# One layer of a hybrid decoder trunk: ones' products among the first products, recurrent outputs by tokens, and a last operand made between products

## The chip, the cores and the metric

The kernel runs on one core of a Trainium2 chip. Times are microseconds (us) on the device, from launch to end; the time of a kernel is the median of its runs. The engines are TensorE (PE; PEld is its loading of weights), VectorE (DVE), ScalarE (ACT), GpSimd (POOL) and SyncE (SP), which issues most transfers.

## The reference

Input x has 1024 tokens of 1024 channels, float32; there is one layer. In short:

```
u    = rms_norm(x)
proj = u @ w_in                          # q, k, v: 8 heads of 64; hq, hf, hi, hg: 4 heads of 128
attn = rms_norm(three dilated windows of causal attention, merged by their sums)
# recurrence, per head, in chunks: forget = lb + (1-lb)*sigmoid(hf); key = 1-forget; b = cumsum(log forget)
A       = causal(q*exp(b) @ (key*exp(-b)).T)
o       = A @ hi + (q*exp(b)) @ state;   state = exp(b_end)*state + (key*exp(b_end-b)).T @ hi
rec  = rms_norm(o, over the 128 channels of a head) * silu(hg)
h    = x + concat(attn, rec) @ w_out
g, v = rms_norm(h) @ w_up                # 2 x 2816 columns
h    = h + (gelu(causal conv of width 3 over g) * v) @ w_down
out  = rms_norm(h)
```

## The kernel before, in words

**Layout.** Most tensors lie with channels on the 128 partitions and tokens along the row: 8 channel blocks of 1024 tokens, worked in two halves of 512 tokens. To hold float32 accuracy each operand of a large product is split into an upper part in a shortened format and the lower rest, so that one product becomes three: upper by upper, upper by lower, lower by upper.

**Weights.** `Ring` (L48) brings weights in pieces of 128x512 in the order of a plan: a transfer by SP into one of five raw buffers, the upper part by ACT (L86), the lower part by POOL or, for keys listed in `ring.on_vector`, by DVE (both L88). Five split pieces live at a time; `done` frees one and starts the next.

**Order.** PE's instructions run in the order in which the program writes them. The other engines' queues are ordered by a planner that uses the written order and its own costs, except where an instruction is pinned (`keep_in_program_order`, `pin`). Work is woven by hand: generators yield a product's price in us, and `Fill.run(us)` plays as many products as the credit pays for.

**Stages.**
- *Start.* Eight ones' products (L378), then the queries and keys of heads 0 and 1, `dense` (L445 to L458), channel block by channel block as x arrives and is split by `scale_x` (ACT L390, DVE L391). `rms1` (L404) sums the squares by a ones' product (L406, and L409 by columns); its result R1 scales what comes out of PSUM. For half 1 it is called after the first three value products (`tok`, L460 to L473), and the half-1 copies of queries and keys of heads 0 and 1 (`evac` in `qk_half`, L530 to L546) come at once after it.
- *Attention.* For each head and each pair of 128-token blocks j, `score_steps` makes scores (L575, L576), DVE masks them and finds the maximum (L578), ACT exponentiates (L583), POOL divides (L587); `value_steps` turns them by PE (L602 to L609), splits them (ACT L613, DVE L614) and multiplies by the values (L621 to L625). Beside each head run weight products from `beside`; the loop's `cost[h]` says how many us of them a head gets.
- *Recurrence.* `recur` (L838 to L914) is one turn for one head and one half: five steps, eight turns, played between the products of hf, hq and hg at places given by `steps` in units of 5.2 us. Step 1 makes the cumulative sums and exponentials; step 2 turns B (psK, L865) and makes psA (L870 into the lower 64 rows, L873 into the upper); step 3 makes psU (L882) and the states; step 4 makes the outputs psO (L901, L903), channels by tokens, and their squares; step 5 sums the squares over the channels by a ones' product (L908), takes the root (`rstd_part`, L325 to L332, on 128x512) and multiplies by the gate (L910 on DVE, L912 on POOL).
- *Output product.* `out_pair` (L990 to L1026): two of eight output blocks at a time, PSUM banks of the tag mm, two in number; DVE adds x (L1014). The second norm (`norm2`, L1038) runs between.
- *Up.* Column blocks 0 and 1 are plain. From block 2 on, `up` (L1220) makes a block by seven products instead of eight (a Strassen-Winograd form): the activations' operands b11, b21, b22 and T1 to T4 are made once, the weights' s1 to s4 per block on DVE by `Mix`. T4, the operand that meets a22, is made by `sum_4` (L1176) and `split` (L1158) before block 2.
- *Down.* The same form over ten pairs of blocks, then the final norm.

PSUM has eight banks: the tags mm, s, o and t with two each until the up stage.

Of the kernel before, what the change touches and what calls it, by code (L numbers as in the profile page):

```python
# [22 lines left out]
NH = 8  # L23
# [179 lines left out]
def hybrid_kernel(ctx: ExitStack, tc: tile.TileContext, xT, w_qk, w_tok, w_hg, w_out, w_up,  # L203
# [173 lines left out]
    for _ in range(8):  # L377
        PE.matmul(warm[:, :P], ones, ones, start=True, stop=True)  # L378
# [66 lines left out]
    def dense(key, hf, evac, last, tag="mm"):  # L445
# [3 lines left out]
        for c in range(NCT):  # L449
            hi, lo = ring.get((key, c // 4))  # L450
            s = slice((c % 4) * P, (c % 4 + 1) * P)
            PE.matmul(ps, hi[:, s], uhi[:, c, t], start=(c == 0), stop=False)
# [66 lines left out]
    if True:  # L519
# [181 lines left out]
        cost = {h: 4.8 * (4 if h in (5, 6) else 3) for h in range(NH)}  # L701
        for h in range(NH):
            fill.add(*beside[h])
            for j in range(4):
# [7 lines left out]
                k = 0  # L712
                while True:
# [5 lines left out]
                    if not got or k % 2:  # L719
                        more = next(va, 0)  # L720
# [23 lines left out]
    with pool("hg", "right") as hg:  # L744
# [93 lines left out]
        def recur(h, hf):  # L838
# [29 lines left out]
            for c in range(4):  # L868
                s, s1 = slice(c * P, (c + 1) * P), slice(c * P, c * P + 64)
                PE.matmul(psA[0:64, s], B[:, s1], E[:, s], start=True, stop=True)  # L870
            for c in range(4):
                s, s2 = slice(c * P, (c + 1) * P), slice(c * P + 64, (c + 1) * P)
# [7 lines left out]
            for c in range(4):  # L880
# [3 lines left out]
            DVE.tensor_mul(U, psU.rearrange("p (c v) -> p c v", c=4), ex[:, 8:12].unsqueeze(2).to_broadcast([P, 4, P]))  # L884
# [5 lines left out]
            for c in range(1, 4):  # L890
                DVE.scalar_tensor_tensor(U[:, c], U[:, c - 1], ex[:, 4 + c : 5 + c], U[:, c], op0=ALU.mult, op1=ALU.add)
# [4 lines left out]
            yield  # L896
            psO = bank("o", f"psO{nm}")
            for c in range(4):
                s = slice(c * P, (c + 1) * P)
                no_state = hf == 0 and c == 0  # L900
                PE.matmul(psO[:, s], iv[:, 4 * hf + c, h * P : (h + 1) * P], AT[:, c], start=True, stop=no_state)  # L901
# [3 lines left out]
            ACT.activation(sq, psO, AF.Square)  # L905
            yield
            ss = bank("t", f"hss{nm}")
            PE.matmul(ss, ones, sq, start=True, stop=True)  # L908
            R = rstd_part(ht("rs_y", f"rhy{nm}"), ht("rs_m", f"rht{nm}"), ss, 1.0 / P)
            DVE.scalar_tensor_tensor(R, psO, col(V_HG + h), R, op0=ALU.mult, op1=ALU.mult)  # L910
            g_ = G[h, hf]
            POOL.tensor_mul(g_, R, g_)  # L912
# [38 lines left out]
        for n, (h, hf) in enumerate(((0, 0), (0, 1), (1, 0), (1, 1), (2, 0), (3, 0), (2, 1), (3, 1))):  # L951
# [3 lines left out]
            steps += zip((start, at, at + 1, at + 2.2, at + 3.1), rec_steps(h, hf))  # L955
# [34 lines left out]
        def out_pair(hf, d0):  # L990
# [217 lines left out]
    for c in range(KS):  # L1208
        sum_4(c)
    T[4] = operand(1, KS, "b12")  # L1210
    for c in range(KS):
        split(T[4][c], uf1[c])
    ps1_cm.__exit__(None, None, None)

    with pool("ps2", "left", space=PSUM) as ps2:
# [4 lines left out]
        def up(f, sums):  # L1220
# [6 lines left out]
            for i in (1, 2, 5, 6, 7, 4, 3) if f == 2 else (1, 5, 6, 7, 2, 3, 4):  # L1227
# [31 lines left out]
        sums = iter(())  # L1259
# [234 lines left out]
```

## Time and profile before

| what | value |
|---|---|
| median of 3 runs | 1224.47 us (1224.36 to 1224.59) |
| the profiled execution's own time | 1229.3 us |
| its span, first to last instruction | 1227.1 us |
| PE busy | 1205.3 us, 98% of the span |
| DVE busy | 964.7 us, 79% |
| ACT busy | 633.2 us, 52% |
| POOL busy | 309.1 us, 25% |
| mean granted clock of TensorE | 0.993 |

In a row of the waits stand who waited, for whom, the total, the count and the longest. In a row of the windows stand the stretch, its length, then for each engine asked for the busy time with the instructions in brackets, the granted clock, the transfers' share and GB/s. In a row of the timeline stand the start, the duration, the engine and line, what is written from what, sizes, the count, and in brackets the idle time before it with what ended it. In the chain of waits stand the start, the part on the chain and the instruction. The profiler models the ends of products: a 128x512 product is shown with 0.39 us while the next starts after 0.23.

### The profile page before, as it was taken

How to read it: one execution, taken by the hardware profiler on the slowest of the kernel's cores; microseconds unless marked ns; L12 is line 12 of the kernel's file. 1: busy time of each engine (PE TensorE's matmuls, PEld its weight loads, DVE VectorE, ACT ScalarE, POOL GpSimd, SP SyncE). 2: the span in 40 equal slices, each digit the busy share in tenths (PEclk: the TensorE clock that was granted, in tenths of full speed). 3: DMA queues.
4: the chain of work that ended last, by engine and by line, in shares of the span. 5: the costliest groups of instructions: out<-in, count | busy, mean ns of one | idle time of the engine just before them, and what ended most of it. 6: DMA issues, size and time to landing. Idle time of an engine off the chain costs nothing.

```text
span 1227.1 us, 17373 instructions
## 1 busy us (share of the span) xinstructions
PE 1205.3 (98%) x5992; PEld 1012.3 (82%) x5992; DVE 964.7 (79%) x1788; ACT 633.2 (52%) x1149; POOL 309.1 (25%) x286
## 2 busy tenths in 40 slices
PE   8999999999999999999999999999999999999996
PEld 7898888888888888878878888888888888888886
DVE  7867776666778877474988988988988879957996
ACT  7466667667656656454633334334434354444553
POOL 1154446555011024513212223122222210000000
PEclk9999999999999999999999999999999999999998
DMA  6121112123111112343012233332233257434522
GB/s 235 42 70 53 52 53 78 60 65 111 52 35 48 57 60 96 120 137 112 26 61 88 93 109 117 118 111 80 102 112 120 104 173 264 155 104 154 172 96 94
DMA packets 71816, 122.38 MB, mean 100 GB/s; under 512 B 7344, under 2 KB 17840, under 8 KB 71728
## 3 DMA queue, kind: packets, MB, share of 16 engines
q1 hardware_dynamic: 60928, 101.80, 25.8%
q10 hardware_dynamic: 10800, 19.47, 4.1%
q8 instruction: 47, 0.77, 0.3%
q14 instruction: 41, 0.34, 0.1%
HBM read 97.65 MB, written 23.59 MB: 99 GB/s over the span
## 4 chain that ended last, share of the span: by engine, by line
PE 90%; DVE 4%; issue 2%; ACT 2%; DMA 0%; POOL 0%; SPq 0%; DVEq 0%; ACTq 0%; POOLq 0%
PE p L1105 10%; PE p L1104 10%; PE p L1103 10%; PE ds L1394 3%; PE ds L1392 3%; PE ds L1393 3%; PE da L1394 2%; PE da L1392 2%; PE da L1393 2%; PE po L1007 2%; PE po L1009 2%; PE po L1008 2%; PE piv L504 1%; PE S L575 1%; PE piv L506 1%
## 5 line engine op out<-in xcount | busy, mean ns | idle before, releaser
L88 POOL TENSOR_TENSOR wlo<-raww,whi 128x512 fp32r<-128x512 f32 x141 | 206.7, 1477 | 388.7 <-ACT whi L86 259.5
L86 ACT CAST whi<-raww 128x512 fp32r<-128x512 f32 x276 | 167.8, 617 | 188.1 <-DVE raww L120 61.5
L88 DVE TENSOR_TENSOR wlo<-raww,whi 128x512 fp32r<-128x512 f32 x136 | 100.1, 736 | 18.2 <-ACT whi L86 18.0
L86 ACT CAST whi<-r 128x512 fp32r<-128x512 f32 x70 | 43.6, 623 | 83.0 <-PE ds L1393 49.7
L587 POOL TENSOR_SCALAR P<-P,st 128x512 f32<-128x512 f32 (+2 forms) x96 | 55.7, 591 | 112.8 <-DVE st L584 65.7
L578 DVE CUSTOM_DVE_ANT_0 P<-S,mask 128x512 f32<-128x512 f32 (+2 forms) x96 | 52.0, 553 | 28.0 <-PE S L576 27.2
L583 ACT ACTIVATE P<-P,st 128x128 f32<-128x128 f32 (+3 forms) x64 | 49.7, 776 | 33.8 <-DVE st L582 17.0
L614 DVE TENSOR_TENSOR tl<-T,th 128x512 fp32r<-128x512 f32 (+1 forms) x80 | 50.8, 635 | 18.2 <-ACT th L613 17.0
L88 DVE TENSOR_TENSOR wlo<-r,whi 128x512 fp32r<-128x512 f32 x70 | 47.9, 685 | 18.7 <-ACT whi L86 18.5
L1394 PE MATMUL ds<-fhi,wlo 128*128 128x512 f32 x160 | 62.3, 389 | 0.0
L1393 PE MATMUL ds<-flo,whi 128*128 128x512 f32 x160 | 62.3, 389 | 0.0
L1392 PE MATMUL ds<-fhi,whi 128*128 128x512 f32 x160 | 62.2, 389 | 0.0
L1103 PE MATMUL p<-b1h,whi 128*128 128x512 f32 x160 | 62.2, 389 | 0.0
L1104 PE MATMUL p<-b1l,whi 128*128 128x512 f32 x160 | 62.2, 389 | 0.0
L1105 PE MATMUL p<-b1h,wlo 128*128 128x512 f32 x160 | 62.2, 389 | 0.0
L1132 ACT ACTIVATE cv<-cv 128x512 f32<-128x512 f32 x44 | 27.8, 633 | 61.6 <-DVE cv L1125 61.4
L1366 POOL TENSOR_TENSOR facc<-facc,sqf 128x256 f32<-128x256 f32 x4 | 2.9, 737 | 222.8 <-ACT sqf L1365 222.8
L1125 DVE SCALAR_TENSOR_TENSOR cv<-g,vec,cv 128x511 f32<-128x511 f32 (+2 forms) x92 | 55.0, 603 | 4.7 <-ACT cv L1122 3.7
L613 ACT CAST th<-T 128x512 fp32r<-128x512 f32 (+1 forms) x80 | 43.0, 537 | 22.3 <-PE T L606 17.9
L88 DVE TENSOR_TENSOR flo<-rawf,fhi 128x512 fp32r<-128x512 f32 x70 | 47.9, 684 | 3.7 <-ACT fhi L86 3.7
L86 ACT CAST fhi<-rawf 128x512 fp32r<-128x512 f32 x70 | 43.2, 617 | 14.6 <-DMA rawf<-spT 5.6
L1392 PE MATMUL da<-fhi,whi 128*128 128x512 f32 x120 | 46.7, 389 | 0.0
(669 smaller groups left out, 3864.2 us busy)
## 6 DMA issues: line engine op xcount, KB each, us to landing
raww<-in_w_up_dram SPq DMA_DIRECT2D x88, 256.0 KB, 3.1
raww<-in_w_tok_dram SPq DMA_DIRECT2D x52, 256.0 KB, 2.6
rawf<-spT SPq DMA_DIRECT2D x40, 256.0 KB, 2.7
r<-in_w_down_dram SPq DMA_DIRECT2D x40, 256.0 KB, 3.2
raww<-in_w_hg_dram SPq DMA_DIRECT2D x32, 256.0 KB, 2.6
raww<-in_w_out_dram SPq DMA_DIRECT2D x32, 256.0 KB, 2.6
spB<-a ACTq DMA_DIRECT2D x30, 256.0 KB, 2.3
spT<-t ACTq DMA_DIRECT2D x30, 256.0 KB, 2.0
```

The costliest lines, as they stand in the source:

```text
L86: self.pin(self.high(hi[:, :w], raw))
L88: self.pin(low.tensor_sub(lo[:, :w], raw, f32(hi[:, :w])))
L578: DVE.tensor_tensor_reduce(Pt[:, k0 : k0 + w], S[:, :w], mask[:, m : m + w], -1.0, BIG * 3, op0=ALU.add, op1=ALU.min, accum_out=st[:, k0 / ...
L587: POOL.tensor_scalar(e, e, st[:, 3:4], 1.0, op0=ALU.mult, op1=ALU.mult)
L614: DVE.tensor_sub(tl[:, :n], T[:, :n], f32(th[:, :n]))
L1103: PE.matmul(ps, hi[:, s], bhi, start=(start and n == 0), stop=False)
L1104: PE.matmul(ps, hi[:, s], blo, start=False, stop=False)
L1105: PE.matmul(ps, lo[:, s], bhi, start=False, stop=(stop and n == len(rhs) - 1))
L1125: DVE.scalar_tensor_tensor(dst, x, col(V_CW + j * NFF + f), dst, op0=ALU.mult, op1=ALU.add)
L1392: PE.matmul(ps[d], hi[:, s], ahi, start=(k == 0), stop=False)
L1393: PE.matmul(ps[d], hi[:, s], alo, start=False, stop=False)
L1394: PE.matmul(ps[d], lo[:, s], ahi, start=False, stop=(k == NPAIR - 1))
```

## The change

- *Start.* Ones' products are put among the first products of queries and keys: four after the first product of channel block 0 of head 0, one after its third, two after the first of channel block 1.
- *Half 1's sum.* The scores of head 0, block pair 0, and the fourth value product come ahead of `rms1(1)`. The copies of the half-1 queries and keys of heads 0 and 1 move into the loop of head 0, at block pairs 0 and 1.
- *Last head.* Its share of weight products is 12.8 us instead of 14.4, and 1.6 us are played ahead of its last block pair.
- *Recurrence.* In psA the products into lower and upper rows alternate chunk by chunk. In half 1 the fourth chunk of psU, which nothing reads, is left out. The outputs come with tokens on the partitions (operands swapped); ACT sums the squares along the row, four instructions of 128 columns with a sum each; the root is taken on 128x4; DVE multiplies; at step 5 four transposes turn the result, and DVE multiplies by weight and gate. Step 5 moves from 3.1 to 3.7 units.
- *Banks.* In half 1 the output blocks 0 and 1 use the tag s, 2 and 3 the tag o, 6 and 7 the tag s.
- *Block 2.* T4 is made one channel block after each of the first four products. The product with a22 comes last and the one with s4 sixth, in the ring's plan as well.

```diff
-            xs = ("a11", "a12", "s1", "s2", "s3", "a22", "s4") if f == 2 else ("a11", "s1", "s2", "s3", "a12", "s4", "a22")
+            xs = ("a11", "a12", "s1", "s2", "s3", "s4", "a22") if f == 2 else ("a11", "s1", "s2", "s3", "a12", "s4", "a22")
...
+    def busy(n):
+        for _ in range(n):
+            PE.matmul(warm[:, :P], ones, ones, start=True, stop=True)
+
+    busy(8)
+
+    between = {(("qk", 0), 0, 0): (4, 1), (("qk", 0), 0, 1): (2, 0)}
...
+            b = between.get((key, hf, c), (0, 0))
             PE.matmul(ps, hi[:, s], uhi[:, c, t], start=(c == 0), stop=False)
+            busy(b[0])
             PE.matmul(ps, hi[:, s], ulo[:, c, t], start=False, stop=False)
             PE.matmul(ps, lo[:, s], uhi[:, c, t], start=False, stop=(c == NCT - 1))
+            busy(b[1])
...
-        rms1(1)
-        for g in pairs[1]:
-            next(g, None)
...
+        for Ps in score_steps(0, 0):
+            pass
+        fill.add(v0[3])
+        fill.run()
+        rms1(1)
...
-        fill.add(v0[3])
-        fill.run()
-        for Ps in score_steps(0, 0):
-            pass
         fill.add(v0[4])
...
         cost = {h: 4.8 * (4 if h in (5, 6) else 3) for h in range(NH)}
+        cost[NH - 1] = 12.8
...
+                if (h, j) == (NH - 1, 3):
+                    fill.run(1.6)
...
+                        if h == 0 and k == 1 and j < 2:
+                            next(pairs[1][j], None)
                         more = next(va, 0)
...
                 PE.matmul(psA[0:64, s], B[:, s1], E[:, s], start=True, stop=True)
-            for c in range(4):
-                s, s2 = slice(c * P, (c + 1) * P), slice(c * P + 64, (c + 1) * P)
                 PE.matmul(psA[64:128, s], B[:, s2], E[:, s2].unsqueeze(1).to_broadcast([P, 2, 64]), start=True, stop=True)
...
-            for c in range(4):
+            n = 3 if hf else 4
+            for c in range(n):
                 s = slice(c * P, (c + 1) * P)
                 PE.matmul(psU[:, s], kT[:, s], iv[:, 4 * hf + c, h * P : (h + 1) * P], start=True, stop=True)
...
-                PE.matmul(psO[:, s], iv[:, 4 * hf + c, h * P : (h + 1) * P], AT[:, c], start=True, stop=no_state)
+                PE.matmul(psO[:, s], AT[:, c], iv[:, 4 * hf + c, h * P : (h + 1) * P], start=True, stop=no_state)
                 if not no_state:
-                    PE.matmul(psO[:, s], st[:, c], E[:, s], start=False, stop=True)
-            sq = ht("rs_m", f"hsq{nm}")
-            ACT.activation(sq, psO, AF.Square)
+                    PE.matmul(psO[:, s], E[:, s], st[:, c], start=False, stop=True)
+            sq, ss = ht("rs_m", f"hsq{nm}"), hg.tile([P, 12], F32, tag="sm", name=f"hss{nm}", bufs=2)
+            for c in range(4):
+                s = slice(c * P, (c + 1) * P)
+                ACT.activation(sq[:, s], psO[:, s], AF.Square, accum_out=ss[:, c : c + 1])
+            R = rstd_part(ss[:, 4:8], ss[:, 8:12], ss[:, 0:4], 1.0 / P)
+            on = ht("rs_y", f"on{nm}")
+            DVE.tensor_mul(on.rearrange("p (c v) -> p c v", c=4), psO.rearrange("p (c v) -> p c v", c=4),
+                           R.unsqueeze(2).to_broadcast([P, 4, P]))
             yield
-            ss = bank("t", f"hss{nm}")
-            PE.matmul(ss, ones, sq, start=True, stop=True)
-            R = rstd_part(ht("rs_y", f"rhy{nm}"), ht("rs_m", f"rht{nm}"), ss, 1.0 / P)
-            DVE.scalar_tensor_tensor(R, psO, col(V_HG + h), R, op0=ALU.mult, op1=ALU.mult)
+            psT = bank("t", f"psT{nm}")
+            for c in range(4):
+                s = slice(c * P, (c + 1) * P)
+                PE.transpose(psT[:, s], on[:, s], ident)
             g_ = G[h, hf]
-            POOL.tensor_mul(g_, R, g_)
+            DVE.scalar_tensor_tensor(g_, psT, col(V_HG + h), g_, op0=ALU.mult, op1=ALU.mult)
...
-            steps += zip((start, at, at + 1, at + 2.2, at + 3.1), rec_steps(h, hf))
+            steps += zip((start, at, at + 1, at + 2.2, at + 3.7), rec_steps(h, hf))
...
-                    ps[d] = bank("mm", f"po{hf}_{d}")
+                    ps[d] = bank({(1, 0): "s", (1, 2): "o", (1, 6): "s"}.get((hf, d0), "mm"), f"po{hf}_{d}")
...
-    for c in range(KS):
-        sum_4(c)
     T[4] = operand(1, KS, "b12")
-    for c in range(KS):
-        split(T[4][c], uf1[c])
+
+    def last_sums():
+        for c in range(KS):
+            sum_4(c)
+            split(T[4][c], uf1[c])
+            yield
...
-            for i in (1, 2, 5, 6, 7, 4, 3) if f == 2 else (1, 5, 6, 7, 2, 3, 4):
+            for i in (1, 2, 5, 6, 7, 3, 4) if f == 2 else (1, 5, 6, 7, 2, 3, 4):
...
-        sums = iter(())
+        sums = last_sums()
```

More of the change, by code (lines that the diff above doesn't have):

```diff
@@ L376, in hybrid_kernel @@
     warm = bank("mm", "warm")
-    for _ in range(8):
-        PE.matmul(warm[:, :P], ones, ones, start=True, stop=True)
+    def busy(n):
[3 more added lines that the diff above has]
+    between = {(("qk", 0), 0, 0): (4, 1), (("qk", 0), 0, 1): (2, 0)}
     pin = tc.keep_in_program_order
@@ L868, in recur @@
             for c in range(4):
-                s, s1 = slice(c * P, (c + 1) * P), slice(c * P, c * P + 64)
+                s, s1, s2 = slice(c * P, (c + 1) * P), slice(c * P, c * P + 64), slice(c * P + 64, (c + 1) * P)
                 PE.matmul(psA[0:64, s], B[:, s1], E[:, s], start=True, stop=True)
-            for c in range(4):
-                s, s2 = slice(c * P, (c + 1) * P), slice(c * P + 64, (c + 1) * P)
                 PE.matmul(psA[64:128, s], B[:, s2], E[:, s2].unsqueeze(1).to_broadcast([P, 2, 64]), start=True, stop=True)
@@ L883, in recur @@
             U = ht("rs_m", f"U{nm}").rearrange("p (c t) -> p c t", c=4)
-            DVE.tensor_mul(U, psU.rearrange("p (c v) -> p c v", c=4), ex[:, 8:12].unsqueeze(2).to_broadcast([P, 4, P]))
+            DVE.tensor_mul(U[:, :n], psU[:, : n * P].rearrange("p (c v) -> p c v", c=n),
+                           ex[:, 8 : 8 + n].unsqueeze(2).to_broadcast([P, n, P]))
             st = ht("rs_y", f"st{nm}").rearrange("p (c t) -> p c t", c=4)
@@ L890, in recur @@
             for c in range(1, 4):
-                DVE.scalar_tensor_tensor(U[:, c], U[:, c - 1], ex[:, 4 + c : 5 + c], U[:, c], op0=ALU.mult, op1=ALU.add)
+                if c < n:
+                    DVE.scalar_tensor_tensor(U[:, c], U[:, c - 1], ex[:, 4 + c : 5 + c], U[:, c], op0=ALU.mult, op1=ALU.add)
                 DVE.tensor_scalar_mul(st[:, c], U[:, c - 1], ex[:, c : c + 1])
```

## The prediction

> **What bounds the kernel now.** I read the page's head and its chain of work first, then what TensorE waits for, then short windows around those waits, then the recurrence's instructions one by one.
>
> ```profile
> span 1227.1 us, 17373 instructions
> PE 1205.3 (98%) x5992; PEld 1012.3 (82%) x5992; DVE 964.7 (79%) x1788; ACT 633.2 (52%) x1149; POOL 309.1 (25%) x286
> ...
> PE 90%; DVE 4%; issue 2%; ACT 2%; DMA 0%; POOL 0%; SPq 0%; DVEq 0%; ACTq 0%; POOLq 0%
> ```
>
> TensorE (PE) is busy for 98% of the span and makes 90% of the chain that ends last. So a microsecond taken out of PE's own queue is a microsecond off the time, as long as its operands come in time; work taken from another engine is worth nothing by itself. The second view lists what PE waits for (total us, times, longest).
>
> ```profile
> PE p L1105 <- POOL wlo L88: 2.4, 2, 2.2
> PE p__qk___0_0_211 L452 <- ACT uhi L390: 1.4, 1, 1.4
> PE ss L406 <- DVE sq L402: 1.4, 1, 1.4
> PE po L1007 <- DVE h L1014: 1.3, 1, 1.3
> PE T L602 <- DVE tl L614: 1.1, 1, 1.1
> PE T L603 <- POOL P L587: 0.9, 1, 0.9
> ```
>
> These six waits, 8.5 us, are each touched by an edit. Windows (length, PE busy, granted clock) show what else they cost:
>
> ```profile
> 5.30:8.70 3.40, 1.39 (x4) 1.00 0.98 338
> 8.70:12.20 3.50, 3.21 (x9) 0.51 1.04 393
> 42.90:46.30 3.40, 2.38 (x15) 1.00 0.04 7
> 46.30:49.70 3.40, 3.40 (x18) 0.50 0.00 0
> 551.40:554.90 3.50, 2.18 (x11) 1.00 0.33 107
> 630.00:633.40 3.40, 1.16 (x5) 1.00 0.00 0
> 633.40:636.80 3.40, 3.40 (x9) 0.50 0.49 155
> ```
>
> Three of the waits are each followed by 3.4 us at half clock. Half of 3.4 us is lost: 1.7 us a spell. The fourth wait, 1.3 us at 551, fell in a window with 2.18 us of work and was not punished. In the window from 42.9 the 2.38 us include eight one-column products (0.95 us); without them 1.43 us remain. So on this trace the clock fell after windows with 1.2 to 1.4 us of full products and held after one with 2.2.
>
> The Trainium skill (TensorE: Matmul & The Clock Gate, "What's actually happening") ties the cold state to at least one idle window of about 3.4 us. Here it came after waits of 1.4 to 2.4 us, so the trace disagrees; if idle windows alone decided, these spells would not hang on the waits, and would stay (a rival below).
>
> **The change part by part.**
>
> *Ones' products at the start.*
>
> ```profile
> 1.05 3.78 PE L378 MATMUL warm<-ones 128*128 128x128 f32 x16 [1.05 <-DVE ones L229]
> 12.41 0.39 PE L452 MATMUL p__qk___0_0_211<-uhi,whi 128*128 128x512 f32 x1
> ```
> ```profile
> 9.52 1.45 DVE L391 SCALAR_TENSOR_TENSOR ulo<-xt,vec,uhi 128x512 fp32r<-128x512 f32 x2
> ```
>
> The eight products that are there take 3.78 us as 16 instructions, 0.24 each. Seven more are 14 instructions, 1.5 us at full clock and 3.3 at half. They stand where PE waits for the first pieces of x, in a window that has 2.0 us free (3.40 - 1.39), so I cost them at nothing; the loss end is 3.3 - 2.0 = 1.3 us, all of them at half clock. They lift the window's 1.39 us of work to about 2.4 us (0.9 + 0.2 of ones after the first channel block, part of 0.4 after the second). That is above the 2.18 that kept the clock: the spell goes. PE's first product after the wait is at 9.0, so the spell costs (12.2 - 9.0)/2, about 1.5 us. The operands can follow: the lower part of channel block 2 is done by 11.0, where its product starts at 12.4 today. Gain **1.5** (-1.3 to 1.5).
>
> *Sums of squares later.* The ones' product that waits for DVE's sums (1.4 us) is moved behind block (0,0)'s scores and the fourth value product, 24 products of 256 columns, 0.12 each (half of a full one's 0.23, in the recurrence's chain below), so 2.9 us of PE work that cover the 1.4; the spell from 46.3 goes with it. Behind it come R1, the second half's queries and keys of head 0 and 1, moved into the loop of head 0, and the value copies, all on DVE and ACT, no transfers. Gain 1.4 + 1.7 = **3.1** (0 to 3.1). Head 0's first transposes wait 0.9 us for POOL; they start on earlier scores, but the moved copies now stand between, so I take half, **0.5** (-1 to 0.9).
>
> *Value products of the last head.* With a share of 12.8 instead of 14.4, 1.6 us of weight products are left for the place of the wait at 295. I take the wait's **1.1** (0 to 1.1).
>
> *Recurrence, eight turns.* Its chain:
>
> ```profile
> 357.25 0.86 PE hss L908 x2
> ...
> 375.50 0.44 PE psK L865 x4
> 375.94 0.69 PE psA L870 x5
> 376.96 0.49 PE psA L873 x5
> 377.45 1.06 PE hss L908 x2
> 378.51 0.23 PE p__hg___1_0_4384 L452
> ...
> 383.97 0.89 PE psU L882 x8
> ```
> ```profile
> 375.87 0.76 PE L870 MATMUL psA<-E,B 128*64 128x128 f32 x5
> 376.37 0.32 PE L873 MATMUL psA<-E,B 128*64 128x128 f32 x1
> ...
> 376.74 0.71 PE L873 MATMUL psA<-E,B 128*64 128x128 f32 x5
> ```
>
> The sum of squares over a head's channels by a ones' product costs 0.86 us of PE; four transposes of the same size as psK's cost 0.44. 8 x 0.42 = **3.4** saved. psU loses one of four chunks in half 1: 2 of 8 instructions of 0.89 us, 0.22, in four turns: **0.9**. The outputs by tokens swap the operands of products whose sizes stay (128x128), so they cost the same. In psA the products into the upper 64 rows already run beside those into the lower 64: the first L873 starts at 376.37, before L870 is through, but 0.50 us after L870's first, for it stands behind eight of them. In alternate order it stands behind two. Five of L870 start within 0.76 - 0.27 = 0.49 us, 0.12 a step, so behind two is 0.12 to 0.25; I take 0.16. That is 0.34 saved a turn, 8 x 0.34 = **2.7**. The loss end is no overlap: 16 x 0.11 (psK's) = 1.76 us against today's 1.42 (from 375.87 to the last start, 377.18, and 0.11), so +0.34 a turn.
>
> What can eat this is a new wait: the transposes need the normalised outputs, which go through ACT and DVE.
>
> ```profile
> 348.70 0.44 PE psO L901 x4
> ```
> ```profile
> 353.21 0.58 ACT L905 ACTIVATE hsq<-psO 128x512 f32<-128x512 f32 x1
> ...
> 359.58 0.68 ACT L327 ACTIVATE rht<-hss,eps 128x512 f32<-128x512 f32 x1
> ```
> ```profile
> 365.42 0.75 DVE L910 SCALAR_TENSOR_TENSOR rhy<-psO,vec,rhy 128x512 f32<-128x512 f32 x1
> ```
>
> Today the squares start about 3.0 us after psO's 14 products end at 350.2, and from the logarithm to the product's end are 6.6 us, queueing included. Four squares with sums I put at 1.6 us (0.4 each, an estimate from the 0.58 of the wide one), and five operations on 4 columns instead of 512 save some 0.4 each, 2.0: 3.0 + 1.6 + 4.6 = 9.2 us. The time there is: 1.5 steps of 5.2 us = 7.8, and the next turn's psK and psA between, 1.6: 9.4. That is a tie, so I take off 0.25 us a turn, **-2.0** (0 to -20.8: 3.0 + 2.4 + 6.6 = 12.0 without any saving, 2.6 us late). A late transpose holds up everything on PE behind it, the gate products above all. ACT gets no more work (0.58 + 3 x 0.68 = 2.6 before; 1.6 + 3 x 0.28 = 2.4 after), and the gate's product leaves POOL, with its 1.4 us, for DVE:
>
> ```profile
> L912 POOL TENSOR_TENSOR G<-rhy,G 128x512 f32<-128x512 f32 x7 | 10.0, 1435 | 81.5 <-DVE rhy L910 81.5
> ```
>
> DVE does two wide operations a turn after it (the normalising one, and the gate's) where it had three, so it is not the loser.
>
> *Banks.* The output products of half 1 get banks of their own for d 0 to 3, so the product at 553 no longer waits for DVE's addition in the middle of norm 2: **1.3** (0 to 1.3; the next use of an old bank is two pairs, 22 us, later).
>
> *Block 2's last operand.*
>
> ```profile
> 628.60 2.49 DVE L1160 TENSOR_TENSOR b12l<-uf,b12h 128x512 fp32r<-128x512 f32 x4
> ...
> 637.09 0.69 DVE L115 TENSOR_TENSOR raww<-raww,raww 128x512 f32<-128x512 f32 x1 [3.72 <-DMA raww<-in_w_up_dram]
> ```
> ```profile
> 629.24 0.62 ACT L86 CAST whi<-raww 128x512 fp32r<-128x512 f32 x1
> ```
> ```profile
> 629.93 2.89 POOL L88 TENSOR_TENSOR wlo<-raww,whi 128x512 fp32r<-128x512 f32 x1 [22.76 <-DVE b12l L1160]
> ```
> ```profile
> 600.00:616.00 16.00, 16.00 (x72) 13.26 (x71) 16.00 (x25) 7.50 (x13) 5.60 (x2) 1.00 0.14 50
> 616.00:640.00 24.00, 21.76 (x88) 17.28 (x87) 19.49 (x34) 8.55 (x15) 4.39 (x2) 0.93 0.20 67
> ```
>
> The sixth product's weights a22 are late: their upper part stands in ACT's queue behind the four pieces of T4, and POOL's lower part comes at 632.8. After the change a22 comes seventh, and T4's pieces stand between products of 2.7 us (12 x 0.23). DVE is full before it (16.00 of 16.00) and T4's last piece ends at 628.60 + 2.49 = 631.1. With s4's two operations (the sum and the lower part, 1.4 us) now ahead of it, that becomes 632.5. The sixth product could start at 629.9, when a22's upper part was there, so the seventh starts at 629.9 + 2.7 = 632.6. It just fits, piece by piece. What is late next is block 3's first mixed weights (the DVE row at 637.09, behind a transfer whose buffer a22 frees; a22 is split earlier now). Gain 2.4 + 1.7 = **4.1** (0 to 4.1).
>
> Sum: 1.5 + 3.1 + 0.5 + 1.1 + 3.4 + 0.9 + 2.7 - 2.0 + 1.3 + 4.1 = **16.6 us**. The profiled execution took 1229.3 us (span 1227.1 and 2.2 around it), so it would be 1212.7; the median of the runs is 4.8 lower, 1224.5, and the same difference gives **1207.9 us**.
>
> **Rivals.**
> *The wait moves to T4 (chance 0.12).* DVE is full there; if its queue puts T4 behind the additions of products 5 and 6 (three more, 1.8 us) and the seventh product waits 2 us, the clock falls again: the 4.1 are lost, 1212.0. For it: 16.00 of 16.00. Against: DVE sat idle 3.72 us at 637.
> *The clock is not held (0.12).* The ones do not count as enough work, or idle windows alone decide: one to three spells stay, 1.5 to 4.9 us, 1209.4 to 1212.8. Against: windows of 1.4 and 2.2 us of work fell on different sides.
> *psA's halves do not overlap when alternated (0.08).* 2 x 2.7 = 5.4: 1213.3. Against: the two rows that interleave at 376.4 to 376.7.
> *The transposes wait (slower, 0.05).* At recurrence step +3.7 PE stands for 2.6 us in each of eight turns: 18.6 gained elsewhere, 20.8 lost, 1226.7. It decides from 2.3 us a turn. For it: the 3.0 us before the squares and the 6.6 after the logarithm. Against: wide operations become narrow, and one ones' product leaves the chain.
> *Nothing happens (0.03).* Other engines' queues fall into another order and give all back: 1224.
>
> **How the numbers follow.** The forecast has 0.55 (1202.5 to 1211), two rivals at once 0.05 (to 1217). All terms at their good ends give 1203.5 (0.4 more at head 0, 2.0 at the transposes). The range 1202.5 to 1216 holds forecast and the single rivals, 0.87. A change under 0.2% (2.4 us) cannot be told from none here; faster by more 0.92, same 0.03, slower 0.05.
>
> **What would show it.** Right: clock 1.00 in the windows 8.7 to 12.2, 46.3 to 49.7 and after block 2; no PE wait on sq, on h or on wlo; L873 starting within 0.2 us of L870; no row of psT waiting for `on` above 0.3 us. Wrong: such a row with over 2 us a turn, a wait on b12 in block 2, or a half-clock window where none was.

## The result, and the profile after

The changed kernel takes **1211.64 us** (median of 4 runs, 1210.85 to 1212.4) against 1224.53 us (1224.36 to 1226.41, 4 runs) for the kernel before: ratio 0.9891, interval 0.9874 to 0.9908. The forecast was 1207.9 us with a range of 1202.5 to 1216. So the sign was right and the time lies in the range, 3.7 us above the forecast. The profiled execution of the changed kernel took 1211.85 us, near its median; the first profiled one of the kernel before took 1229.3, 4.8 above its own.

Line numbers from here on are those of the changed kernel: L380 is the ones' product (L378 before), L459, L461 and L462 the large products (L452 to L454), L584 and L587 scores and mask (L575, L578), L591 the negated maximum, L592 and L596 exponential and division (L583, L587), L611 to L615 the transposes of attention, L882 and L883 psA (L870, L873), L930 the new transposes psT.

The page of the changed kernel, its head and the head of its chain of work:

```profile
span 1209.9 us, 17468 instructions
PE 1193.9 (99%) x6014; PEld 1006.8 (83%) x6014; DVE 951.6 (79%) x1792; ACT 627.2 (52%) x1205; POOL 299.2 (25%) x278
...
PE 93%; issue 2%; DVE 2%; ACT 1%; POOL 0%; DMA 0%; SPq 0%; DVEq 0%; ACTq 0%; POOLq 0%
```

TensorE (PE) lost 11.4 us of busy time with 22 instructions more, and 5.8 us of not being busy. What it still waits for (total us, times, longest):

```profile
PE T L612 <- POOL P L596: 2.6, 1, 2.6
...
PE p L1125 <- POOL wlo L88: 0.5, 1, 0.5
```

The waits on sq and on h are gone, that on wlo in block 2 shrank from 2.4 to 0.5, and no row names psT, the tile of the new transposes. The first row is new: head 0's transposes wait 2.6 us for POOL, where it was 0.9. Windows of the changed kernel (length, PE busy, granted clock, transfers):

```profile
5.30:8.70 3.40, 3.04 (x20) 1.00 0.96 319
8.70:12.20 3.50, 3.50 (x17) 1.00 1.05 401
...
46.30:49.70 3.40, 3.40 (x28) 1.00 0.00 0
...
60.00:63.40 3.40, 0.77 (x7) 1.00 0.22 77
63.40:66.80 3.40, 3.40 (x15) 0.50 0.22 77
```

The half-clock spells at 8.7, 46.3 and after block 2 are gone, and there is one where there was none: at 63.4, behind the new wait. The prediction had named that as a sign of being wrong.

Where the time went, by the start of one marked product per stage in the timelines. "Before again" is a second profiled execution of the kernel before (1224.99 us, the first experiment below). The forecast's terms are those of the prediction, put to these stages.

| stage, from one marked product to the next | before | before again | after | after minus before / before again | forecast |
|---|---|---|---|---|---|
| start to the first sum of squares | 24.68 | 24.56 | 22.55 | -2.1 / -2.0 | -1.5 |
| to head 2's queries and keys (sum of squares, head 0) | 57.63 | 56.11 | 56.63 | -1.0 / +0.5 | -3.6 |
| to the first product of hf (last head) | 222.70 | 222.62 | 221.75 | -0.9 / -0.9 | -1.1 |
| to the first up product (recurrence, banks) | 267.07 | 267.18 | 257.77 | -9.3 / -9.4 | -6.3 |
| to the first down product (block 2) | 429.73 | 427.37 | 425.84 | -3.9 / -1.5 | -4.1 |
| to the end of the span | 225.33 | 225.33 | 225.34 | 0.0 / 0.0 | 0 |
| span | 1227.14 | 1223.17 | 1209.88 | -17.3 / -13.3 | -16.6 |

Against the execution on which the sum was made, the sum was right within 0.7 us, with two large errors of opposite sign in it. Against the second execution of the kernel before, 3.4 us of it were not there to be had.

### The profile page after: what moved, and what is told of

The parts are those of the page before. It is cut to its first block, busy times and chain, and to the rows that moved or that the text cites. A ratio compares the mean times of both kernels' runs of the same rounds, so it can differ in the third digit from the quotient of the medians.

```text
span 1209.9 us, 17468 instructions
## 1 busy us (share of the span) xinstructions
PE 1193.9 (99%) x6014; PEld 1006.8 (83%) x6014; DVE 951.6 (79%) x1792; ACT 627.2 (52%) x1205; POOL 299.2 (25%) x278
## 4 chain that ended last, share of the span: by engine, by line
PE 93%; issue 2%; DVE 2%; ACT 1%; POOL 0%; DMA 0%; SPq 0%; DVEq 0%; ACTq 0%; POOLq 0%
PE p L1125 10%; PE p L1123 10%; PE p L1124 10%; PE ds L1418 3%; PE ds L1417 3%; PE ds L1416 3%; PE po L1027 2%; PE po L1029 2%; PE po L1028 2%; PE da L1418 2%; PE da L1417 2%; PE da L1416 2%; PE S L584 1%; PE piv L513 1%; PE S L585 1%
## 5 line engine op out<-in xcount | busy, mean ns | idle before, releaser
L88 DVE TENSOR_TENSOR wlo<-raww,whi 128x512 fp32r<-128x512 f32 x136 | 97.4, 716 | 22.6 <-ACT whi L86 22.5
L596 POOL TENSOR_SCALAR P<-P,st 128x512 f32<-128x512 f32 (+2 forms) x96 | 56.3, 596 | 110.8 <-DVE st L593 62.2
L587 DVE CUSTOM_DVE_ANT_0 P<-S,mask 128x512 f32<-128x512 f32 (+2 forms) x96 | 52.1, 553 | 29.9 <-PE S L585 29.0
L592 ACT ACTIVATE P<-P,st 128x128 f32<-128x128 f32 (+3 forms) x64 | 49.7, 776 | 32.9 <-DVE st L587 16.6
L623 DVE TENSOR_TENSOR tl<-T,th 128x512 fp32r<-128x512 f32 (+1 forms) x80 | 50.7, 634 | 16.6 <-ACT th L622 15.6
```

The costliest lines, as they stand in the source:

```text
L88: self.pin(low.tensor_sub(lo[:, :w], raw, f32(hi[:, :w])))
L587: DVE.tensor_tensor_reduce(Pt[:, k0 : k0 + w], S[:, :w], mask[:, m : m + w], -1.0, BIG * 3, op0=ALU.add, op1=ALU.min, accum_out=st[:, k0 / ...
L596: POOL.tensor_scalar(e, e, st[:, 3:4], 1.0, op0=ALU.mult, op1=ALU.mult)
L623: DVE.tensor_sub(tl[:, :n], T[:, :n], f32(th[:, :n]))
```

## The experiments

The ratio of each run is to executions of the kernel before that were taken beside it. Their medians lie between 1224.5 and 1226.0 us from one experiment to the next, so differences of about 1 us between two experiments are read from the profiles, not from the times.

### before_again: the kernel before, unchanged, in many runs

> The kernel before, unchanged, run and profiled again. Its profile took 1229.3 us, its timed runs 1224.5; after the change both agree (1211.85 and 1211.6). Theory 1 (the half-clock spells depend on how the clock's 3.4 us windows lie over the waits, so an execution has all, some or none of the three): the granted clock differs between executions, a new profile lies between 1222 and 1229 us, and an execution's time goes with its number of half-clock spells, 1.5 to 1.7 us each; timed runs of 1224.5 would have a clock of 0.995 or more against the 0.993 of the first profile. Theory 2 (profiling itself costs this kernel 4.8 us): the new profile takes 1229 us again at a clock of 0.993, and timed runs of 1224.5 have the same clock.

Measured: 1225.24 us (1223.9 to 1228.2, 11 runs) against 1225.09 (1222.91 to 1227.25, 15 runs), ratio 1.0004 (0.9995 to 1.0014). The kernel before spreads over 5 us. Its second profile (line numbers of the kernel before) has the same waits as the first, shorter in block 2 and at the start:

```profile
PE p L1105 <- POOL wlo L88: 1.7, 2, 1.2
PE ss L406 <- DVE sq L402: 1.4, 1, 1.4
```

but not the same half-clock spells. Windows of that second profile, around the sum of squares and block 2:

```profile
42.30:45.70 3.40, 2.04 (x13) 1.00 0.00 0
45.70:49.10 3.40, 3.40 (x30) 1.00 0.03 7
...
629.40:632.80 3.40, 2.65 (x11) 1.00 0.43 141
632.80:636.20 3.40, 3.40 (x16) 1.00 0.06 18
```

So two of the three spells, 1.7 us each, come in one execution and not in another. Theory 2 has fallen, since this profile took 1224.99. The mean granted clock of the 47 executions of the kernel before that list it is 0.996 in the median; three have 0.993 like the first profile, three 0.998 like this one. The changed versions' profiles have 0.996 or 0.997 with one such spell and 0.997 or 0.998 with none, so by its clock an ordinary execution of the kernel before has one such spell or none. The third stretch at half clock, at the start, is there, longer even. Rows of the second profile's timeline:

```profile
12.51 0.59 PE L454 MATMUL p__qk___0_0_211<-uhi,wlo 128*128 128x512 f32 x1
12.94 0.40 PE L452 MATMUL p__qk___1_0_218<-uhi,thw 128*128 128x512 f32 x1
13.18 0.39 PE L453 MATMUL p__qk___1_0_218<-ulo,thw 128*128 128x512 f32 x1
```

Until 12.9 the products start 0.43 us apart, from then on 0.24.

### after_again: the changed kernel once more

> The changed kernel, unchanged, run and profiled again beside the others. If half-clock spells are a matter of how the clock's windows lie, the wait of 2.6 us at head 0's transposes stays in this profile, while the spell behind it may or may not appear; with it the span is 1209 to 1210, without it 1207.5 to 1208.5. The time is 1211.6 within 1 us.

Measured: 1211.46 us (1211.17 to 1212.87, 4 runs) against 1226.01 (1224.23 to 1227.98, 7 runs), ratio 0.988 (0.9863 to 0.9896). In its profile the transposes again wait 2.6 us for POOL, and a half-clock spell follows (63.2 to 66.6); in block 2 the waits are longer than in the first profile of this kernel:

```profile
PE p L1125 <- POOL wlo L88: 0.7, 1, 0.7
PE p L1125 <- DVE wlo L88: 0.5, 1, 0.5
```

So the new wait is the kernel's own, and the rest that is left in block 2 varies between 0.5 and 1.2 us.

### no_mid: the second sum of squares and the copies put back

```diff
-        for Ps in score_steps(0, 0):
-            pass
-        fill.add(v0[3])
-        fill.run()
         rms1(1)
+        for g in pairs[1]:
+            next(g, None)
...
+        fill.add(v0[3])
+        fill.run()
+        for Ps in score_steps(0, 0):
+            pass
...
-                        if h == 0 and k == 1 and j < 2:
-                            next(pairs[1][j], None)
```

> The changed kernel with the second sum of squares and the copies of the half-1 queries and keys back at their old places. In the changed profile a new wait of 2.6 us at 60 us (head 0's transposes for POOL) and a half-clock spell behind it took the place of the old wait of 1.4 us at 44 us and its spell. Theory 1 (the wait only moved): head 2's first weight product starts within 1 us of 79.2 us and the time stays within 1 us of 1211.6. Theory 2 (the forecast, 3.1 us saved): 82.3 us and 1214.7.

Measured: 1210.8 us (1209.96 to 1212.85), ratio 0.9886 (0.9871 to 0.9901), so not slower than with the edit. In its profile head 2's queries and keys start at 77.48 instead of 79.18 (82.3 was forecast); 0.4 of the difference lies ahead of the first sum of squares, so the edit cost 1.3 us there. Its waits:

```profile
PE ss L412 <- DVE sq L408: 1.1, 1, 1.1
...
PE T L612 <- POOL P L596: 0.9, 1, 0.9
```

The moved sum of squares hides 1.1 us as meant; the copies moved with it make the transposes wait 1.7 us longer and bring the spell.

### copies_later: the same edit with head 1's copies further back

```diff
-                        if h == 0 and k == 1 and j < 2:
+                        if h == 0 and (j, k) in ((0, 1), (1, 3)):
                             next(pairs[1][j], None)
```

> The changed kernel with head 1's half-1 copies written after the scores of block pair 2 of head 0 instead of before its second half. In the changed profile head 0's transposes at 59.8 us wait 2.6 us for POOL because DVE makes head 1's copies (54.3 to 58.4 us) between the masks of those scores. If that is the cause, the wait falls under 0.8 us, the half-clock spell from 63.4 us goes, and the time falls by 2.5 to 4 us, to 1207.5 to 1209. Rival (ACT and POOL are full in this ramp whatever the order): the wait stays within 1 us and the time within 1 us.

Measured: **1208.56 us** (1208.13 to 1209.14), ratio 0.9863 (0.9849 to 0.9876). No spell is left in its profile, and the wait falls to about what it was (under 0.8 was expected):

```profile
PE T L612 <- POOL P L596: 1.0, 1, 1.0
```

The cause stands in the changed kernel's timeline, here of DVE, ACT, POOL and PE in turn:

```profile
54.31 0.69 DVE L548 TENSOR_TENSOR x<-p__qk___1_1_272,R 128x512 f32<-128x512 f32 x1
...
56.95 0.67 DVE L587 CUSTOM_DVE_ANT_0 P<-S,mask 128x512 f32<-128x512 f32 x1
...
57.66 0.77 DVE L554 TENSOR_TENSOR kl<-x,kh 64x512 fp32r<-64x512 f32 x1
...
58.47 0.42 DVE L587 CUSTOM_DVE_ANT_0 P<-S,mask 128x256 f32<-128x256 f32 x1
...
59.29 1.13 DVE L591 TENSOR_TENSOR st<-st 128x1 f32<-128x1 f32 x1
...
60.51 0.94 ACT L592 ACTIVATE P<-P,st 128x768 f32<-128x768 f32 x1 [1.47 <-DVE st L591]
...
59.12 1.28 POOL L88 TENSOR_TENSOR wlo<-raww,whi 128x512 fp32r<-128x512 f32 x1 [0.45 <-ACT whi L86]
61.92 1.14 POOL L596 TENSOR_SCALAR P<-P,st 128x512 f32<-128x512 f32 x2 [1.52 <-DVE st L593]
...
62.66 0.33 PE L612 MATMUL T<-ident,P 128*128 128x128 f32 x1 [2.63 <-POOL P L596]
```

Head 1's copies (L548 to L554) stand on DVE ahead of and between the two masks of the second token block of block pair 2 (512 and 256 columns wide), whose exponential and division PE waits for. The second mask comes at 58.47; one place later for the copies, it comes at 56.24. A second thing adds to it: the one-column operation at 59.29 takes 1.13 us, where the same one at 54.92 takes 0.15, and ends (60.42) as POOL's lower part of a weight does (59.12 + 1.28 = 60.40). The Trainium skill (SBUF — State Buffer, "SBUF: two separate sides") says that a VectorE operation with two SBUF inputs and a GpSimd operation that reads SBUF share a port pair under an exclusive lock; these rows agree.

### no_t4: block 2's last operand made ahead, as before

```diff
-            xs = ("a11", "a12", "s1", "s2", "s3", "s4", "a22") if f == 2 else ("a11", "s1", "s2", "s3", "a12", "s4", "a22")
+            xs = ("a11", "a12", "s1", "s2", "s3", "a22", "s4") if f == 2 else ("a11", "s1", "s2", "s3", "a12", "s4", "a22")
...
+    for c in range(KS):
+        sum_4(c)
     T[4] = operand(1, KS, "b12")
...
-    def last_sums():
...
-        for c in range(KS):
-            sum_4(c)
-            split(T[4][c], uf1[c])
-            yield
...
+    for c in range(KS):
+        split(T[4][c], uf1[c])
...
-            for i in (1, 2, 5, 6, 7, 3, 4) if f == 2 else (1, 5, 6, 7, 2, 3, 4):
+            for i in (1, 2, 5, 6, 7, 4, 3) if f == 2 else (1, 5, 6, 7, 2, 3, 4):
...
-        sums = last_sums()
+        sums = iter(())
```

> The changed kernel with T4 made before block 2 again and a22 ahead of s4. Block 2 (from its first product to block 3's) took 23.35 us in the first profile of before (a wait of 2.4 us and a half-clock spell), 20.6 in the second (a wait of 1.4, no spell) and 19.9 after the change. Theory 1 (the edit is worth the wait alone; the spell is chance): block 2 takes 20.3 to 21 us without a spell, 22.5 to 23.5 with one, and the time is 0.7 to 1.5 us longer in most executions. Theory 2 (the forecast, 4.1 us each time): 23.3 us or more and 3.5 us longer.

Measured: 1214.17 us (1213.27 to 1216.09), ratio 0.991 (0.9895 to 0.9925). The time, 2.5 us longer than the changed kernel's, lies between the two theories (0.7 to 1.5, and 3.5), and block 2 takes 23.3 us, as both allow with a spell. The wait for the weights is back with 2.2 us, and in this profile the spell behind it; but the 2.6 us wait of head 0, which this version has too, was not punished here. Windows of its profile, laid in steps of 3.41 us from the border at 617.51, where its clock fell:

```profile
57.78:61.20 3.42, 1.96 (x12) 1.00 0.01 2
61.20:64.61 3.41, 2.17 (x16) 1.00 0.28 74
614.10:617.51 3.41, 1.26 (x5) 1.00 0.00 0
617.51:620.93 3.42, 3.34 (x8) 0.50 0.43 153
```

The wait fell over a border, and both windows kept 2 us of work. This run was meant for block 2 and shows the clock's rule as well (below).

### j2_t4late: copies at block pairs 0 and 2, last operand one product later

```diff
-                        if h == 0 and k == 1 and j < 2:
-                            next(pairs[1][j], None)
+                        if h == 0 and k == 1 and j in (0, 2):
+                            next(pairs[1][j // 2], None)
...
-                next(sums, None)
+                if f > 2 or i != 1:
+                    next(sums, None)
```

> Not a step back but a trial of two causes at once: head 1's half-1 copies written in block pair 2 of head 0 (later still than in copies_later, which left a wait of 1.0 us at head 0's transposes), and T4's pieces written after the second to fifth product of block 2 instead of the first to fourth, so that a22's cast need not queue behind the last piece on ACT (b12 at 613.74, a22 at 614.27 in copies_later). If both causes are right, the wait for POOL at 59.5 us and the one at block 2's last product (0.5 us) both fall under 0.3 us and the time is 1207 to 1208. Rival (the planner orders these by readiness, whatever the written order): waits and time as in copies_later, 1208.6.

Measured: 1209.31 us (1208.17 to 1209.55), ratio 0.9865 (0.9849 to 0.9882). The copies are out of the way here too; block 2 is no better:

```profile
PE T L612 <- POOL P L596: 1.1, 1, 1.1
...
PE p L1125 <- POOL wlo L88: 0.6, 1, 0.6
PE p L1125 <- DVE wlo L88: 0.5, 1, 0.5
```

The second edit, the later T4, did not reach the queues: ACT makes T4's pieces 9.45, 11.86 and 15.48 us after block 2's first product here and 9.45, 11.86 and 15.47 in after_again. So the rival held, and the run does not tell what a later T4 is worth. In the changed kernel the upper part of the late weight stands on ACT right behind T4's last piece, POOL's lower part follows at 618.47, and PE waits for that one and not for T4:

```profile
617.25 0.62 ACT L1179 CAST b12h<-uf 128x512 fp32r<-128x512 f32 x1 [1.39 <-DVE uf L1201]
617.77 1.67 ACT L86 CAST whi<-raww 128x512 fp32r<-128x512 f32 x3
...
620.34 0.50 PE L1125 MATMUL p<-b12h,wlo 128*128 128x512 f32 x1 [0.54 <-POOL wlo L88]
```

That this queue is what remains is read from the rows; in no version that was run did it have another order.

### no_psA: all lower products of psA first, as before

```diff
                 PE.matmul(psA[0:64, s], B[:, s1], E[:, s], start=True, stop=True)
+            for c in range(4):
+                s, s2 = slice(c * P, (c + 1) * P), slice(c * P + 64, (c + 1) * P)
                 PE.matmul(psA[64:128, s], B[:, s2], E[:, s2].unsqueeze(1).to_broadcast([P, 2, 64]), start=True, stop=True)
```

> The changed kernel with psA's products in the old order (four into the lower rows, then four into the upper). If alternating them lets both halves run side by side, the old order costs 0.34 us a turn, 2.7 us in eight turns, in the stretch from the first hf product to the second norm's sum (220.5 us after the change, so 223.2), and as much in the time. Rival (it gains nothing, the whole saving of the recurrence came from the ones' products): under 0.8 us.

Measured: 1214.98 us (1213.38 to 1215.96), ratio 0.9914 (0.9899 to 0.9928). From hf's first product to the up stage its profile takes 261.51 us instead of 257.77: 3.74, or **0.47 a turn** (0.34 forecast). One turn in the changed kernel's timeline:

```profile
369.48 0.60 PE L877 MATMUL psK<-ident,B 128*128 128x128 f32 x4
370.00 0.32 PE L882 MATMUL psA<-E,B 128*64 128x128 f32 x1
370.01 0.32 PE L883 MATMUL psA<-E,B 128*64 128x128 f32 x1
...
370.82 0.27 PE L882 MATMUL psA<-E,B 128*64 128x128 f32 x1
370.83 0.27 PE L883 MATMUL psA<-E,B 128*64 128x128 f32 x1
371.03 0.50 PE L459 MATMUL p__hg___1_0_4406<-uhi,whi 128*128 128x512 f32 x1
```

The halves start together, 0.01 us apart, a pair every 0.12 us. In no_psA's profile the same turn has its first product into the upper rows 0.49 us behind the first into the lower ones (371.00 and 370.51).

### no_tokens: outputs by channels, squares summed by the ones' product

```diff
-                PE.matmul(psO[:, s], AT[:, c], iv[:, 4 * hf + c, h * P : (h + 1) * P], start=True, stop=no_state)
+                PE.matmul(psO[:, s], iv[:, 4 * hf + c, h * P : (h + 1) * P], AT[:, c], start=True, stop=no_state)
...
-            psT = bank("t", f"psT{nm}")
-            for c in range(4):
-                s = slice(c * P, (c + 1) * P)
-                PE.transpose(psT[:, s], on[:, s], ident)
+            ss = bank("t", f"hss{nm}")
+            PE.matmul(ss, ones, sq, start=True, stop=True)
...
-            steps += zip((start, at, at + 1, at + 2.2, at + 3.7), rec_steps(h, hf))
+            steps += zip((start, at, at + 1, at + 2.2, at + 3.1), rec_steps(h, hf))
```

> The changed kernel with the recurrence's outputs channels by tokens again: the ones' product of 0.86 us in place of four transposes of 0.44, step 5 back at 3.1. If the transposes wait for nothing, as the changed profile says, the old form costs 8 x 0.42 = 3.4 us in the stretch from the first hf product to the second norm's sum (220.5 us after the change, so 223.9). Rival (the transposes carry hidden costs, such as switching or waits under the profile's threshold): under 2 us.

Measured: 1216.34 us (1213.76 to 1218.02), ratio 0.9924 (0.9907 to 0.9941). The same stretch takes 262.76 us: 4.99 more. 3.4 of it are the ones' products against the transposes (8 x 0.42); 1.0 are waits that neither the kernel before nor the changed one shows:

```profile
PE psO L917 <- DVE st L905: 0.8, 2, 0.4
...
PE psO L917 <- DVE st L901: 0.2, 1, 0.2
```

The last 0.6 stay unassigned. So the edit is worth 3.4 us or more; the rival (under 2) has fallen.

### no_banks: one tag for all output blocks, as before

```diff
-                    ps[d] = bank({(1, 0): "s", (1, 2): "o", (1, 6): "s"}.get((hf, d0), "mm"), f"po{hf}_{d}")
+                    ps[d] = bank("mm", f"po{hf}_{d}")
```

> The changed kernel with all output products in the two banks mm again. Forecast: the wait for DVE's addition in the middle of norm 2 (1.3 us, a gap of 1.5 us in PE's starts) comes back, so the stretch from the second norm's first sum to block 0's first product goes from 37.25 to 38.6 us, or the one before it by as much, and the time rises by 1.3 to 1.5 us. Rival (with the recurrence shorter, DVE is ahead and the wait is gone anyway): under 0.4 us.

Measured: 1213.04 us (1211.61 to 1214.5), ratio 0.9894 (0.9879 to 0.9908), against 1211.46 and 0.988 of after_again, which shares its executions of the kernel before. The wait is back, and the stretch from the second norm to the up stage takes 38.84 us instead of 37.25, 1.6 more (1.3 forecast):

```profile
PE po L1027 <- DVE h L1034: 1.3, 1, 1.3
```

### no_ones: no ones' products among the first ones

```diff
-    between = {(("qk", 0), 0, 0): (4, 1), (("qk", 0), 0, 1): (2, 0)}
+    between = {}
```

> The changed kernel without the seven ones' products between the first products. If they hold the clock as forecast, a half-clock spell comes back at 8.7 to 12.2 us and the ones' product of the first sum of squares starts 1.5 us later than after the change (24.1 instead of 22.55); the time is 1.5 us longer (1213.1). Rival: the transfers of x set the pace and the place of the spell is chance; then under 0.5 us.

Measured: 1211.46 us (1211.01 to 1215.58, 5 runs), ratio 0.9896 (0.9881 to 0.991), the same as with them. In its profile no spell came at the start (the one at head 0 did), and the first sum of squares starts at 21.48 instead of 22.55. So where the clock holds anyway, the seven products cost up to 1 us. Two of the five executions took 1213.7 and 1215.6, at a mean clock of 0.995; whether it fell at their start is not shown.

### fill_shift: copies_later, with the beside-work of head 0 moved to the wait

```diff
+        cost[0] = 12.0
...
+                if (h, j) == (0, 2):
+                    fill.run(1.5)
...
-                        if h == 0 and k == 1 and j < 2:
+                        if h == 0 and (j, k) in ((0, 1), (1, 3)):
```

> copies_later, and in head 0 the weight products are shared out at 12.0 us instead of 14.4, with 1.5 us of them played ahead of block pair 2, whose transposes still waited 1.0 us for POOL. If that wait only lacks work to hide it, it falls under 0.4 us and the time is 1207.3 to 1208.0, below copies_later (1208.56) and the changed kernel (1211.64). Rival (products taken from elsewhere open the same wait there, at block pair 1 or 3): time as copies_later within 0.5 us.

Measured: **1207.54 us** (1206.85 to 1208.35), ratio 0.9849 (0.9834 to 0.9864). No wait of head 0's transposes is left, and the window is full:

```profile
60.00:63.40 3.40, 3.40 (x27) 1.00 0.22 77
```

This version is the fastest of those run, 4 us below the changed kernel.

### shift_no_ones: the same without the ones' products

> The version with the copies moved and the fill shifted, without the seven ones' products at the start. Theory 'the ones insure': in most executions the clock holds at the start anyway and the ones cost 0.1 to 0.6 us, but in some a half-clock stretch returns there, so the times of the many executions fall into two groups, most at 1206.5 to 1208 and some 1.5 to 3 us above them; the median stays within 1 us of 1207.5. Rival 'the ones only cost': no upper group, all executions within 1.5 us, median 1207. Rival 'the ones hold the clock': the half-clock stretch is there nearly always, median 1209 to 1210.

Measured: 1207.85 us (1206.8 to 1208.32, 4 runs), ratio 0.9853 (0.9836 to 0.9869), with the edit of no_ones added to fill_shift's. The times lie within 1.5 us, with no upper group. But its profile runs at half clock until 9.5:

```profile
8.77 0.63 PE L459 MATMUL p__qk___1_0_218<-uhi,thw 128*128 128x512 f32 x1
9.20 0.53 PE L461 MATMUL p__qk___1_0_218<-ulo,thw 128*128 128x512 f32 x1
9.56 0.40 PE L462 MATMUL p__qk___1_0_218<-uhi,tlw 128*128 128x512 f32 x1
```

Of four profiles without the added ones three have a half-clock stretch after the first products (the kernel before twice, this one) and one has none (no_ones); of ten with them, none has one beyond 7.0 us. These counts speak for the ones holding the clock; what this is worth in the median, after their own cost, is less than these runs can tell.

## Why the prediction was right or wrong

**Wrong: the base.** "The median of the runs is 4.8 lower, 1224.5, and the same difference gives" 1207.9 us. The 4.8 were not a constant of the profiler: 4.0 of them are the difference of the two spans in the table, and 3.4 of these are the spells that the terms "1.4 + 1.7" and "2.4 + 1.7" took out a second time. An execution without those two spells had no 3.4 us to give. From 1224.99, the second profile, the sum without them is 16.6 - 3.4 = 13.2, which gives 1211.8. By the clocks above an ordinary execution may have one of the two, so the step cost 1.7 to 3.4 us.

**Wrong: "head 0's first transposes", +0.5 in the sum.** The text said that "the moved copies now stand between", and took half a gain. It was a loss: the wait grew from 0.9 to 2.6, and the clock fell behind it. This stage was to give 3.6 (1.9 without the spell) and took 0.5 more than the ordinary execution before. copies_later shows that the place of one generator step is the cause: 3.1 us of the median came back.

**Wrong, and to the good: the -2.0 for the transposes' wait.** "That is a tie" compared 9.2 us with 9.4. Measured, from psO's last product to the end of `on` in the eight turns: 9.3, 7.8, 6.2, 7.6, 5.0, 5.5, 5.6 and 6.7 us. The 9.2 were the worst turn, not the mean, mostly since psO's end, 3.0 us ahead of the squares by the quoted turn, is between 0.1 and 3.4 ahead. The transposes start 1.1 to 4.8 us after `on` is there; PE never waited. The rival "the transposes wait" has fallen.

**Right, with other sizes.** psA: 3.7 instead of 2.7, because the two halves start together and not 0.16 apart; the rival "do not overlap" has fallen. Banks: 1.6 instead of 1.3. Recurrence and banks together: 9.3, where the gross terms without the -2.0 gave 8.3. Of these, 3.7 for psA and 1.6 for the banks leave 4.0 for the tokens and psU, put at 3.4 and 0.9. psU was not run alone. Last head: 0.9 of 1.1. Start: 2.0 to 2.1 instead of 1.5, and the clock held there as forecast. That the ones brought this gain is not shown: in no_ones the clock held without them.

**Right in mechanism, less in amount: T4.** "It just fits" was nearly so: 0.5 to 1.2 us of wait are left of 1.7 to 2.4. What is left is for the lower part of a22: the prediction had it that "a22 is split earlier now", but its upper part still stands behind T4's last piece in ACT's queue. Against the first profile the stage gave 3.9 (forecast 4.1), against the second 1.5. It takes 425.8 us in seven of the eleven profiles with the edit and 426.9 in the other four, so the gain can also be 0.5; without the edit (no_t4) the median is 2.5 longer, and there a spell can follow the wait. The rival "the wait moves to T4" did not come: PE waits for the weight, and no spell follows.

**The rival "the clock is not held"** gave 1209.4 to 1212.8, and the time lies in it, but not for its reason: the three windows it spoke of kept the clock, and a fourth lost it.

The whole account against the forecast: 1207.9, + 3.4 (spells that the second execution has not), + 2.4 (head 0, 1.9 to -0.5), + 0.9 (T4, 2.4 to 1.5), - 3.1 (recurrence and banks, 6.3 to 9.4), - 0.5 (start), + 0.2 (last head) is 1211.2, against 1211.6. That it closes so well owes something to the 3.4, which may be 1.7. One sum of the prediction is off as well: its good ends, 0.4 and 2.0 us better than 1207.9, give 1205.5 and not 1203.5, so the lower end of the range, 1202.5, lies 3 us below what its terms allow.

## What to carry to other kernels

Before a profile's own time is replaced by the median, ask which of the terms are properties of that one execution: a second profile of the unchanged kernel would have shown that two of three spells come and go while their waits stay. When work is moved off one wait, follow each operation that moves with it to the queue where it lands, and list what the bound engine waits for behind that place; here one step of a generator cost 3.1 us. And where a wait falls in the clock's windows differs between executions, so remove the wait rather than count on the spell.

## What the runs showed of the hardware

**Which waits the clock punishes.** The same wait of 2.6 us occurs in seven profiles; six have a spell behind it. The changed kernel's windows stand in the first section; those of no_tokens, cut where its spell begins, are

```profile
60.29:63.70 3.41, 1.43 (x10) 1.00 0.23 77
63.70:67.11 3.41, 3.41 (x17) 0.50 0.27 77
```

The six windows ahead of the spells hold 0.78 to 1.43 us of work, the seventh version's two, shown under no_t4, 1.96 and 2.17. That fits the prediction's reading (the clock fell after 1.2 to 1.4 us and held after 2.2) and narrows it: the border lies between 1.43 and 1.96 of 3.41 us. The ends of the executions, where PE runs out of work, narrow it once more. In copies_later the clock held after a window with 1.56 us:

```profile
1195.40:1198.81 3.41, 1.56 (x6) 1.00 0.37 131
1198.81:1202.22 3.41, 0.00 (x0) 1.00 0.70 247
```

In no_ones it fell after one with 1.03. So by these traces the border is between 1.43 and 1.56 us of work, with the ends of products as the profiler models them and one-column products left out, as in the prediction. What the prediction lacked is that the windows lie where they lie, and a wait that is cut by a border can pass. The Trainium skill (TensorE: Matmul & The Clock Gate, "What's actually happening") calls the window free-running and 3413 ns long, and the rows agree: the spells are 3.41 us long, and where they begin against the same wait differs from profile to profile. Its "idle window" is not needed, since windows with up to 1.43 us of work were enough.

**The first grant of the clock varies.** It came at 12.9 us in one execution of the kernel before and at 9.5 without the ones, with products one behind the other for 3 us and more ahead of it; the clock column of that second profile of the kernel before reads 1.00 from 8.7 to 12.2, where the products' steps of 0.43 us show half. The steps are the surer reading.
